# Inverting triangular blocks in 16x16 pieces, a PSUM bank of its own for preparation, and another order of two output parts in a hybrid decoder layer

## The chip, the cores and the metric

The kernel runs on one core of one Trainium2 chip. A core has a matrix engine (TensorE, "PE" in the profile), three engines for element-wise work (VectorE "DVE", ScalarE "ACT", GpSimd "POOL"), a sync engine that issues transfers (SyncE "SP"), and 16 DMA engines. Each engine works through its own queue in order and waits on semaphores for the others. The metric is the device time of one execution in microseconds; the median of several runs counts.

## The reference

The layer takes x of 256 tokens by 2048 channels, in fp32:

```python
x = LN1(alpha * x + 0.5 * SwiGLU_1(x))                  # 2048 -> 5632 -> 2048
x = LN2(alpha * x + W_out [DiffAttn(x) || RWKV7(x)])    # both from x @ W_in
x = LN3(alpha * x + 0.5 * SwiGLU_2(x))
```

DiffAttn has 8 heads with two score maps each. RWKV7 has 16 heads of size 64 with a state that is updated token by token:

```python
sa = einsum('bhvk,bhk->bhv', state, -kk_t)
state = state * w_t + sa * (kk_t * a_t) + v_t * k_t
y_t = einsum('bhvk,bhk->bhv', state, r_t)
```

After it come a group norm per head, a bonus term and a gate g = sigmoid(x W) g2.

## The kernel before, in words

**Weights.** Every weight matmul is computed in three parts at reduced precision: x and w are each split into a high part and a remainder. SP loads a raw piece of 256 rows by 512 columns (512 KB, L134, three buffers). ScalarE casts it to the high part `wh` (L137), VectorE subtracts to get `wl` (L138), and TensorE runs, for each 128x512 tile, high by high (L113), high by remainder (L114) and remainder by high (L115) into the PSUM tile `acc`. There are five to seven pairs `wh`/`wl` in rotation, and the second half of the tokens lags some pieces behind the first. In all there are 7968 such matmuls ("weight matmuls").

**Background.** The first feed-forward layer, the mixer and the second feed-forward layer follow each other. In the mixer the stream of weight pieces (first W_in, then W_out) carries the rest along: after each piece `run_bg` advances Python generators that emit the small work of RWKV (`rwkv_group`, `rwkv_values`) and attention (`attn_heads`), each with a credit per piece. When a part of W_out needs a result, `drain` runs generators until its own are done. A scheduler with a timeline model then settles the order on each engine; the queues are fixed in the built program.

**RWKV.** The 16 heads go in two groups of 8 (group 0, group 1). For each group: the low-rank decay and learning-rate matmuls with their sigmoids (L500, L501), cumulative sums, key norms with a logarithm and exponentials (L522, L523), the products of key and query sides `BK` and `AR` masked into `Q`; then the inversion. Each head has 4 chunks of 64 tokens, each chunk gives two triangular 32x32 blocks, so there are 64 blocks per group. ScalarE's queue sends them through memory (`dU`) so that one block lies on one partition, on 64 partitions. VectorE inverts them by a recurrence of 31 steps, a multiply (L583) and an add (L585) each. The inverses `Y` and the transposes go back through memory (`dY`, `dYT`) to the layout in which TensorE merges two 32x32 inverses into one of 64x64 (L608, L619; `TT`). L629 transposes `BK`. Then comes the chain of four chunks c = 0 to 3: L642 gives the right side `Rs`, L650 applies the inverse `TT`, L658 updates the state (not for the last chunk), L675 and L681 give the output, L682 copies it to `Yc`. Then the group norm (L696 sums, L700 square, L706 sums, L707 logarithm, L709 exponential, L711 to L716 on VectorE) and the gate (L727, L730, L731). The result is split in high part and remainder (L81, L82) and feeds W_out.

**Output.** `parts` lists the order in which W_out's input rows are taken: 0 and 1 are the halves of attention, 2 and 3 the groups of RWKV. Parts 0 and 2 go together (192 weight matmuls), then part 1 (96), then part 3 (96). After the last one, LN2 is finished; its constants are loaded by GpSimd (L209, L210) into buffers `J1` (that of `SV`, the values) and `Q`.

**PSUM.** Three tags serve the mixer beside `acc`: `at` with two banks (attention, transposes), `sm` with three (everything of RWKV).

Of the kernel before, what the change touches and what calls it, by code (L numbers as in the profile page):

```python
# [16 lines left out]
P = 128  # L17
# [16 lines left out]
BANKS = {"tr": ("at", 2), "sm": ("sm", 3), "at": ("at", 2)}  # L34
# [4 lines left out]
def build(tc, A, out):  # L39
# [49 lines left out]
    class Stream:  # L89
# [78 lines left out]
        def until(self, ready):  # L168
            idle = 0
            while not ready():  # L170
                assert idle < len(self.bg)
                g = self.bg.pop(0)
                try:
                    idle = idle + 1 if next(g) is None else 0
                    self.bg.append(g)
                except StopIteration:
                    pass

        def drain(self, gens):
            self.until(lambda: not any(g in self.bg for g in gens))  # L180
# [149 lines left out]
    def mix(mp, pq, C):  # L330
# [15 lines left out]


# [67 lines left out]
        def rwkv_cols(g, prev=None):  # L415
# [5 lines left out]
            stream.spawn(st["gen"], BG)  # L421

# [18 lines left out]
            return st  # L441
# [14 lines left out]
        def rwkv_values(g, st):  # L456
# [6 lines left out]
            for p in range(4):  # L463
                ps = bank("sm", (P, 4, P))
# [5 lines left out]
            ps = bank("sm", (P, 4, P))  # L470
# [4 lines left out]
            for hf in range(2):  # L475
                ps = bank("sm", (P, 2, S))
# [6 lines left out]
        def rwkv_group(g, st):  # L483
# [7 lines left out]
            for hf in range(2):  # L491
                pw = bank("sm", (P, 2, S))
                pl = bank("sm", (P, 2, S))
                for i in range(2):
                    c0 = (2 * hf + i) * P
                    T.matmul(pw[:, i, :], wa[0:64, c0:c0 + P], lora["tw"][0:64], start=True, stop=True)
                    T.matmul(pl[:, i, :], wa[64:128, c0:c0 + P], lora["tw"][64:128], start=True, stop=True)
                for i in range(2):
                    p = 2 * hf + i
                    SC.activation(out=tl[:, p, :], in_=pw[:, i, :], func=AF.Sigmoid, bias=col(0, g, p))  # L500
                    SC.activation(out=av[:, p], in_=pl[:, i, :].rearrange("p (c t) -> p c t", c=4), func=AF.Sigmoid, bias=col(1, g, p))  # L501
                yield 0.6
# [13 lines left out]
            for hf in range(2):  # L516
                ps = bank("sm", (P, 2, S))
# [32 lines left out]
            for p in range(4):  # L550
                pe = [bank("sm", (P, 4, P)) for e in range(2)]
# [8 lines left out]
            rk = t4("lw")  # L560
            for p in range(4):
# [5 lines left out]
            dY = dp.tile([64, 32, 32], F32, tag="dY", name=nm("dY"))  # L567
            dYT = dp.tile([32, 32, 32], F32, tag="dYT", name=nm("dYT"))
            quad = [(d, e, slice(64 * e + 32 * d, 64 * e + 32 * d + 32), slice(32 * d, 32 * d + 32),
                     slice(32 * d + 16 * e, 32 * d + 16 * e + 16)) for d in range(2) for e in range(2)]  # L570
            for d, e, rr, cc, uu in quad:
                nc.scalar.dma_start(out=dU[uu].rearrange("u s t -> s u t"),
                                    in_=Q[rr, :, :, e, cc].rearrange("p a c t -> p (a c) t"))
            U = hp.tile([64, 32, 32], F32, tag=HT["T1"], name=nm("U"))
            nc.scalar.dma_start(out=U, in_=dU)
            Y = hp.tile([64, 32, 32], F32, tag=HT["T2"], name=nm("Y"))
            V.memset(Y, 0.0)
            V.memset(Y.rearrange("p a b -> p (a b)")[:, ::33], 1.0)
            yield 0.6
            for j in range(31, 0, -1):  # L580
                tmp = mp.tile([64, 256], F32, tag="Rs", name=nm("itmp"))
                tv = tmp[:, 0:j * (32 - j)].rearrange("p (a b) -> p a b", a=j)
                V.tensor_tensor(out=tv, in0=U[:, 0:j, j:j + 1].to_broadcast([64, j, 32 - j]),  # L583
                                in1=Y[:, j:j + 1, j:32].to_broadcast([64, j, 32 - j]), op=ALU.mult)
                V.tensor_tensor(out=Y[:, 0:j, j:32], in0=Y[:, 0:j, j:32], in1=tv, op=ALU.add)  # L585
                if j % 2 == 0:
                    yield 1.0
            V.tensor_copy(out=U, in_=Y.rearrange("p a b -> p b a"))
            nc.scalar.dma_start(out=dY, in_=Y)
            nc.scalar.dma_start(out=dYT, in_=U[0:32])  # L590
            while "values" not in st:
                yield None
            SV = st["SV"]
            TT = hp.tile([P, 16, 64], F32, tag=HT["lw"], name=nm("TT"))
            G.memset(TT, 0.0)
            for d, e, rr, cc, uu in quad:
                nc.scalar.dma_start(out=TT[rr, :, cc], in_=dY[uu].rearrange("u s t -> s u t"))
            YT = hp.tile([P, 16, 32], F32, tag=HT["T1"], name=nm("YT"))
            PT = hp.tile([P, 16, 32], F32, tag=HT["T2"], name=nm("PT"))
            for e in range(2):  # L600
                nc.scalar.dma_start(out=YT[64 * e:64 * e + 32], in_=dYT[16 * e:16 * e + 16].rearrange("u s t -> s u t"))
            yield 0.6
            Qf = Q.rearrange("p a c e t -> p (a c) e t")
# [356 lines left out]
```

## Time and profile before

| | |
|---|---|
| runs | 2024.72, 2017.95, 2019.30 us |
| median | 2019.3 us |
| the profiled execution's own time | 2024.08 us |
| its span in the trace | 2022.2 us |
| TensorE busy | 1977.3 us, 98% |
| VectorE busy | 1147.5 us, 57% |
| ScalarE busy | 883.7 us, 44% |
| GpSimd busy | 35.7 us, 2% |
| mean granted clock of TensorE | 0.984 |

The span runs from the first to the last instruction in the trace; the execution's own time is about 2 us longer. Lines of the profile name the line of the kernel (L113), the engine, the operation, output and input by the program's names, and the shape. "PEld" is TensorE loading the stationary operand, "ACTq" a transfer that ScalarE's queue issued. The bracket at the end of a timeline row is the engine's idle time just before the instruction and what ended it. The granted clock is the share of full speed at which the throttle let TensorE run.

### The profile page before, as it was taken

How to read it: one execution, taken by the hardware profiler on the slowest of the kernel's cores; microseconds unless marked ns; L12 is line 12 of the kernel's file. 1: busy time of each engine (PE TensorE's matmuls, PEld its weight loads, DVE VectorE, ACT ScalarE, POOL GpSimd, SP SyncE). 2: the span in 40 equal slices, each digit the busy share in tenths (PEclk: the TensorE clock that was granted, in tenths of full speed). 3: DMA queues.
4: the chain of work that ended last, by engine and by line, in shares of the span. 5: the costliest groups of instructions: out<-in, count | busy, mean ns of one | idle time of the engine just before them, and what ended most of it. 6: DMA issues, size and time to landing. Idle time of an engine off the chain costs nothing. (4 is left out here: it accounts for less than half of the span.)

```text
span 2022.2 us, 24923 instructions
## 1 busy us (share of the span) xinstructions
PE 1977.3 (98%) x9671; PEld 1623.3 (80%) x9671; DVE 1147.5 (57%) x1419; ACT 883.7 (44%) x1095; POOL 35.7 (2%) x68
## 2 busy tenths in 40 slices
PE   9999999999999999999999988899999999999997
PEld 7888888888888878887777766788888888888886
DVE  5555554445545566775767865755555444555555
ACT  5444433344443335645574443444444334444432
POOL 0200000000000000000000000000000000000000
PEclk9999999999999999999999978999999999999999
DMA  7766666667666656565444624666665666766663
GB/s 243 218 188 195 185 191 209 207 193 229 192 188 188 196 163 196 160 176 163 136 121 141 207 63 154 194 203 187 189 195 185 206 208 198 230 188 189 187 194 129
DMA packets 202009, 373.35 MB, mean 185 GB/s; under 512 B 22827, under 2 KB 24945, under 8 KB 201121
## 3 DMA queue, kind: packets, MB, share of 16 engines
q1 hardware_dynamic: 182928, 350.53, 57.9%
q10 hardware_dynamic: 17440, 14.29, 2.5%
q0 software_dynamic: 1520, 6.93, 1.0%
q8 instruction: 76, 1.25, 0.3%
q14 instruction: 45, 0.36, 0.1%
HBM read 364.10 MB, written 7.60 MB: 184 GB/s over the span
## 5 line engine op out<-in xcount | busy, mean ns | idle before, releaser
L138 DVE TENSOR_TENSOR wl<-raw,wh 128x1024 fp32r<-128x1024 f32 (+1 forms) x665 | 808.0, 1216 | 670.3 <-ACT wh L137 669.3
L137 ACT CAST wh<-raw 128x1024 fp32r<-128x1024 f32 (+1 forms) x665 | 695.4, 1047 | 848.8 <-PE acc L115 733.6
L115 PE MATMUL acc<-wh,xl 128*128 128x512 f32 (+1 forms) x1952 | 741.8, 392 | 0.5 <-DVE xl L82 0.5
L114 PE MATMUL acc<-wl,xh 128*128 128x512 f32 (+1 forms) x1952 | 737.4, 393 | 0.7 <-DVE wl L138 0.7
L113 PE MATMUL acc<-wh,xh 128*128 128x512 f32 (+1 forms) x1952 | 725.5, 392 | 8.5 <-ACT xh L81 5.6
L113 PEld LDWEIGHTS acc<-wh,xh 128*128 128x128 f32 x1952 | 368.9, 189 | 87.5 <-ACT xh L81 7.1
L115 PEld LDWEIGHTS acc<-wh,xl 128*128 128x128 f32 x1952 | 368.9, 189 | 77.2 <-issue 2.0
L114 PEld LDWEIGHTS acc<-wl,xh 128*128 128x128 f32 x1952 | 369.0, 189 | 76.6 <-DVE wl L138 1.8
L115 PE MATMUL acc<-wh,hh 128*128 128x512 f32 x704 | 254.4, 390 | 0.0
L114 PE MATMUL acc<-wl,hh 128*128 128x512 f32 x704 | 253.5, 389 | 0.0
L113 PE MATMUL acc<-wh,hh 128*128 128x512 f32 x704 | 252.8, 389 | 0.0
L114 PEld LDWEIGHTS acc<-wl,hh 128*128 128x128 f32 x704 | 132.2, 188 | 27.6
L113 PEld LDWEIGHTS acc<-wh,hh 128*128 128x128 f32 x704 | 132.1, 188 | 27.4
L115 PEld LDWEIGHTS acc<-wh,hh 128*128 128x128 f32 x704 | 132.2, 188 | 27.3
L243 DVE TENSOR_TENSOR hh<-tr,hh 128x512 fp32r<-128x512 f32 x44 | 30.4, 691 | 64.1 <-ACT hh L242 64.1
L242 ACT CAST hh<-tr 128x512 fp32r<-128x512 f32 x44 | 25.8, 586 | 91.2 <-PE tr L232 91.2
L229 DVE SCALAR_TENSOR_TENSOR h<-sg,acc 128x512 f32<-128x512 f32 x44 | 30.2, 687 | 34.7 <-PE acc L115 34.7
L224 ACT ACTIVATE sg<-acc 128x512 f32<-128x512 f32 x44 | 26.3, 598 | 43.5 <-PE acc L115 43.5
L232 PEld LDWEIGHTS tr<-ident,h 128*128 128x128 f32 x176 | 21.9, 140 | 5.7
L232 PE MATMUL tr<-ident,h 128*128 128x128 f32 x176 | 26.3, 272 | 0.0
L583 DVE TENSOR_TENSOR itmp<-U,Y 64x31 f32<-64x31 f32 (+15 forms) x62 | 20.6, 333 | 4.1 <-DMA U<-dU 2.8
L585 DVE TENSOR_TENSOR Y<-Y,itmp 64x31 f32<-64x31 f32 (+15 forms) x62 | 20.6, 332 | 1.3
(239 smaller groups left out, 753.2 us busy)
## 6 DMA issues: line engine op xcount, KB each, us to landing
raw<-in_ffn_w_up_dram SPq DMA_DIRECT2D x176, 512.0 KB, 3.9
raw<-in_ffn_w_down_dram SPq DMA_DIRECT2D x176, 512.0 KB, 4.3
raw<-in_ffn_w_gate_dram SPq DMA_DIRECT2D x175, 512.0 KB, 3.9
raw<-in_w_in_dram SPq DMA_DIRECT2D x96, 512.0 KB, 3.7
raw<-in_w_out_dram SPq DMA_DIRECT2D x32, 512.0 KB, 4.1
xs<-y ACTq DMA_DIRECT2D x16, 256.0 KB, 3.3
rc<-xs ACTq DMA_DIRECT2D x16, 256.0 KB, 4.4
lng<-in_ln_g_dram POOLq DMA_DIRECT2D x3, 1024.0 KB, 7.8
```

Source lines behind the costliest of these rows:

```text
L113: T.matmul(a, hi, wh[:, j, :w], start=(ki + j == 0), stop=False)
L114: T.matmul(a, hi, wl[:, j, :w], start=False, stop=False)
L115: T.matmul(a, lo, wh[:, j, :w], start=False, stop=(ki + j == last))
L137: SC.copy(out=wh[:, c, :w], in_=raw[:, c, :w])
L138: V.tensor_tensor(out=wl[:, c, :w], in0=raw[:, c, :w], in1=wh[:, c, :w].bitcast(F32), op=ALU.subtract)
L224: SC.activation(out=s, in_=acc, func=AF.Silu)
L229: V.scalar_tensor_tensor(out=h, in0=sg[tt], scalar=0.5, in1=acc, op0=ALU.mult, op1=ALU.mult)
L232: T.transpose(tr[:, i, :], h[:, i * P:(i + 1) * P], ident)
L242: SC.copy(out=hi, in_=tr)
L243: V.tensor_tensor(out=lo, in0=tr, in1=hi.bitcast(F32), op=ALU.subtract)
L583: V.tensor_tensor(out=tv, in0=U[:, 0:j, j:j + 1].to_broadcast([64, j, 32 - j]), in1=Y[:, j:j + 1, j:32].to_broadcast([64, j, 32 - j]), op= ...
L585: V.tensor_tensor(out=Y[:, 0:j, j:32], in0=Y[:, 0:j, j:32], in1=tv, op=ALU.add)
```

## The change

Five things change together.

- Inversion (in `rwkv_group`): the blocks are cut to 16x16 on 128 partitions, so the recurrence has 15 steps (L599, L601 after). The two diagonal 16x16 blocks of each 32x32 block go through memory with runs of 16 numbers, in 2 DMAs for `U`, 4 for `dY` and `dYT` (L607) and 8 back (L613). `dY` and `dYT` are four tensors that GpSimd's queue fills with zeros once at the start of the mixer. TensorE then merges 16x16 to 32x32 by three sets of products (L618 64, L627 32, L633 64 matmuls per group), with copies and one addition around them. The old merges follow as before (L642 and L653 after, L608 and L619 before).
- Banks: `sm` has two banks, and a new tag `pr` one; the low-rank matmuls, the key norms, half of every second `Q` product and the transposes of the values use `pr`.
- Start: `rwkv_start` starts group 1's generator ahead of the attention columns, not with its own columns. The wait for the values stands behind the inversion.
- `drain` advances only the generators that it was asked for, and others only when these cannot go on.
- `parts` is (0, 2), (3,), (1,).

```diff
-BANKS = {"tr": ("at", 2), "sm": ("sm", 3), "at": ("at", 2)}
+BANKS = {"tr": ("at", 2), "sm": ("sm", 2), "pr": ("pr", 1), "at": ("at", 2)}
...
+        def advance(self, g):
+            try:
+                return next(g) is not None
+            except StopIteration:
+                self.bg.remove(g)
+                return True
 
         def drain(self, gens):
-            self.until(lambda: not any(g in self.bg for g in gens))
+            while any(g in self.bg for g in gens):
+                if not any([self.advance(g) for g in gens if g in self.bg]):
+                    assert any([self.advance(g) for g in self.bg if g not in gens])
...
+        zeroed = [[dp.tile([64, 32, 32], F32, tag=f"{n}{g}", name=f"{n}{g}") for n in ("dY", "dYT")] for g in range(2)]
+        zr = mp.tile([64, 256], F32, tag="Rs", name="zr")
+        G.memset(zr, 0.0)
+        for x in (t for z in zeroed for t in z):
+            nc.gpsimd.dma_start(out=x.rearrange("u (q s) t -> u q (s t)", q=4), in_=zr[:, None, :].to_broadcast([64, 4, 256]))
...
-                pw = bank("sm", (P, 2, S))
-                pl = bank("sm", (P, 2, S))
...
+                for k in range(2):
+                    ps = bank("pr", (P, 2, S))
...
-                pe = [bank("sm", (P, 4, P)) for e in range(2)]
+                pe = [bank("sm", (P, 4, P)), bank(("sm", "pr")[p % 2], (P, 4, P))]
...
-            for j in range(31, 0, -1):
...
+            for pp, ss in sub:
+                nc.scalar.dma_start(out=U[pp], in_=dU[:, ss, ss])
...
+            for j in range(15, 0, -1):
...
+            V.tensor_copy(out=YT, in_=Y.rearrange("p a b -> p b a"))
+            for dst, x in ((dY, Y), (dYT, YT)):
+                for pp, ss in sub:
+                    nc.scalar.dma_start(out=dst[:, ss, ss], in_=x[pp])
...
+            for dst, src in ((DT, dYT), (D, dY)):
+                for d, e, rr, cc, uu in quad:
+                    nc.scalar.dma_start(out=dst[rr], in_=src[uu].rearrange("u s t -> s u t"))
+            yield 0.6
+            ps = bank("sm", (P, 16, 32))
+            for u in range(16):
+                for d, e, rr, cc, uu in quad:
+                    T.matmul(ps[rr, u, :], UM[rr, u, :], DT[rr, u, :], start=True, stop=True)
+            V.tensor_tensor(out=PT, in0=ps, in1=C["id32"][:, None, :].to_broadcast([P, 16, 32]), op=ALU.add)
...
+                    T.matmul(ps[r, u, :], D[r, u, :], PT[r, u, :], start=True, stop=True)
+            V.tensor_copy(out=UM[0:32], in_=ps[0:32])
+            SC.copy(out=UM[64:96], in_=ps[64:96])
...
+                    T.matmul(ps[rr, u, :], PT[rr, u, :], D[rr, u, :], start=True, stop=True)
             for d, e, rr, cc, uu in quad:
+                (V.tensor_copy if e else SC.copy)(out=TT[rr, :, cc], in_=ps[rr])
...
-        r1 = rwkv_cols(0)
+        r1 = rwkv_start(0)
+        rwkv_cols(0, r1)
+        r2 = rwkv_start(1, r1)
         a1 = attn_cols(0)
-        r2 = rwkv_cols(1, r1)
+        rwkv_cols(1, r2)
...
-        parts = [(0, 2), (1,), (3,)]
+        parts = [(0, 2), (3,), (1,)]
```

The change moves instructions on every engine. Three places carry the prediction. The first is TensorE's queue at the last weight matmul of output part (0, 2). `sm` and `at` are small PSUM tiles, `k` and `qq` belong to the second attention half. Before, this follows it:

```order
L115 MATMUL acc_9640<-wh_9668,xl_9150 128x512
L619 MATMUL sm_8507<-TT_8441,PT_8448 32x32
L629 MATMUL sm_8544<-ident,BK_7242 128x64 x8
L829 MATMUL at_9414<-ident,ot_9319 128x128 x2
L774 MATMUL at_9441<-k_8144,qq 128x128
L774 MATMUL at_9441<-k_8144,qq 128x256
L619 MATMUL sm_8507<-TT_8441,PT_8448 32x32 x31
L629 MATMUL sm_8554<-ident,BK_7242 128x64 x8
```

After the change the same place reads as follows (L687 is the former L650, L695 the former L658, L712 and L718 the former L675 and L681, L679 the former L642, L832 and L838 attention):

```order
L115 MATMUL acc_9908<-wh_9936,xl_9418 128x512
L687 MATMUL sm_8924<-Rs_8904,TT_8409 64x64 x8
L695 MATMUL sm_8935<-SV_8638,BT_8696 64x64 x4
L695 MATMUL sm_8935<-SV_8638,BT_8697 64x64 x4
L712 MATMUL sm_8968<-Q,SV_8638 64x64 x8
L718 MATMUL sm_8968<-AR_6346,St_8872 64x64 x8
L832 MATMUL at_9822<-ident,s_9717 128x128
```

Before, group 1's merge and its whole chain stood behind the first output part; now the queue is in the third chunk (c = 2) of the chain there, and everything ahead of it stands among weight matmuls.

The second place is the group norm of group 1 and its gate, up to the next weight matmul, on TensorE. Before:

```order
L696 MATMUL sm_8890<-BK_7242,bones 128x256 x2
L696 MATMUL sm_8920<-BK_7242,bones 128x256 x2
L115 MATMUL acc_9831<-wh_9846,xl_9697 128x512
L114 MATMUL acc_9838<-wl_9807,xh_9700 128x512
L115 MATMUL acc_9838<-wh_9806,xl_9701 128x512
L706 MATMUL sm_8925<-BK_7242,bones 128x256 x2
L706 MATMUL sm_8929<-BK_7242,bones 128x256 x2
L727 MATMUL sm_8986<-gs_5667,g_1652_8887 128x256 x2
```

After (L733 is the former L696, L743 the former L706, L764 and L767 the former L727 and L730, L866 the last transpose of an attention head):

```order
L718 MATMUL sm_9027<-AR_6346,St_8944 64x64 x8
L866 MATMUL at_9956<-ident,ot_9872 128x128 x2
L733 MATMUL sm_9048<-BK_6347,bones 128x256 x2
L733 MATMUL sm_9052<-BK_6347,bones 128x256 x2
L866 MATMUL at_9960<-ident,ot_9886 128x128 x2
L743 MATMUL sm_9076<-BK_6347,bones 128x256 x2
L743 MATMUL sm_9080<-BK_6347,bones 128x256 x2
L764 MATMUL sm_9129<-gs_5679,g_1599_9045 128x256 x2
L767 MATMUL sm_9129<-gs_5680,g_1599_9045 128x256 x2
L764 MATMUL sm_9135<-gs_5679,g_1599_9045 128x256 x2
L767 MATMUL sm_9135<-gs_5680,g_1599_9045 128x256 x2
L113 MATMUL acc_9982<-wh_9977,xh_9964 128x512
```

Before, the norm came behind the matmuls of part (1,), with part (3,) waiting for it; now it follows the chain directly, still ahead of both remaining parts.

The third place is ScalarE's queue at the round trip of group 1's inverses through memory. Before:

```order
L589 DMA dY_8063<-Y_8071 64x1024
L137 CAST wh_9668<-raw_9667 128x1024
L590 DMA dYT_8064<-U_8069 32x1024
L597 DMA TT_8441<-dY_8063 32x16x32 x4
L601 DMA YT_8447<-dYT_8064 32x16x32 x2
L811 ACTIVATE ot_9319,ss_9320<-at_9315 128x128 x2
L137 CAST wh_9705<-raw_9704 128x1024
```

After:

```order
L607 DMA dY_5471<-W_8206 64x16x16 x2
L607 DMA dYT_5472<-W_8206 64x16x16 x2
L785 COPY k_8322<-tr_9260 128x4x128
L137 CAST wh_9340<-raw_9339 128x1024
L81 CAST xh_9409<-qq 128x512
L482 COPY SV_8638<-pr_8667 64x4x64
L613 DMA W_8313<-dYT_5472 32x16x32 x4
L613 DMA W_8313<-dY_5471 32x16x32 x4
L137 CAST wh_9358<-raw_9357 128x1024
```

Where one write stood before the loads there are now four writes, some casts and copies, and eight loads; the trip stands earlier in the stream, among the last pieces of W_in's and the first of W_out's columns. On TensorE, L618, the first product of the merge, stands among weight matmuls and waits for these loads; L627 and L633 follow 18 weight matmuls behind it. On GpSimd, the loads of LN2's constants (L207, L208 after) now stand ahead of the last power (L855) of the second attention half, behind all such powers before.

More of the change, by code (lines that the diff above doesn't have):

```diff
@@ L632, in rwkv_group @@
             st["cols"] = True
+            while "values" not in st:
+                yield None
+            SV = st["SV"]
             Yc = be
```

105 lines of the change are left out of this document (51 added, 54 removed).

## The prediction

> **What bounds the kernel now.** I read the spans and clocks first, then the page's busy times, then TensorE's timeline, then a table of busy times by stretch, and last the timeline inside the stretches that came out of line. The span is that of the profiled execution, whose own time is 2024.1 us; the median of the three runs is 2019.3, 0.24% less, so what I work out on the trace is scaled by 2019.3/2024.1 at the end.
>
> ```profile
> core 0: 2022.2 us, clock 0.984
> PE 1977.3 (98%) x9671; PEld 1623.3 (80%) x9671; DVE 1147.5 (57%) x1419; ACT 883.7 (44%) x1095; POOL 35.7 (2%) x68
> 1160.78 0.39 PE L115 MATMUL acc<-wh,xl 128*128 128x512 f32 x1
> 1162.60 0.39 PE L114 MATMUL acc<-wl,xh 128*128 128x512 f32 x1
> 735.00:1063.00 328.00, 321.89 (x1929) 261.42 (x1928) 231.75 (x404) 187.63 (x303) 7.04 (x7) 0.99 0.55 159
> 1063.00:1076.00 13.00, 11.24 (x50) 8.89 (x49) 12.97 (x17) 3.99 (x5) 0.00 (x0) 0.74 0.50 161
> 1164.00:1201.00 37.00, 29.10 (x370) 23.84 (x364) 25.92 (x77) 17.75 (x52) 4.03 (x3) 0.69 0.23 73
> 1201.00:1224.00 23.00, 23.00 (x147) 17.87 (x148) 10.61 (x14) 6.21 (x8) 1.14 (x2) 0.99 0.33 103
> 1224.00:1247.00 23.00, 15.84 (x51) 11.62 (x50) 11.25 (x17) 9.14 (x11) 0.00 (x0) 0.78 0.37 140
> ```
>
> TensorE is the bound: busy 98%, with VectorE at 57% and ScalarE at 44%. Its weight matmuls follow each other every 0.227 us: the two timeline rows are eight matmuls apart, (1162.60 − 1160.78)/8 (a record lasts 0.39, since they overlap). So the time changes in two ways only: TensorE gets more or less to do, or it gets other stretches in which no weight matmul is ready. The rows by stretch (start:end and length, then busy us and records of PE, its weight loads, VectorE, ScalarE, GpSimd, then granted clock, DMA share, GB/s) show three such stretches in the mixer: a short one at 1063, a long one from 1164 to 1201, and one after 1224. Each also has a low granted clock, 0.69 to 0.78 against 0.99.
>
> **The order of the output parts and what remains uncovered.** These rows give the weight matmuls' first stage (L113) alone, then the ends of both stretches.
>
> ```profile
> 1164.00:1201.00 37.00, 0.27 (x1) 0.27 (x1) 0.69 0.23 73
> 1201.00:1224.00 23.00, 11.14 (x28) 5.07 (x28) 0.99 0.33 103
> 1164.04 0.49 PE L115 MATMUL acc<-wh,xl 128*128 128x512 f32 x1
> 1189.14 1.12 PE L650 MATMUL sm<-Rs,TT 64*64 64x64 f32 x16
> 1195.82 0.68 PE L650 MATMUL sm<-Rs,TT 64*64 64x64 f32 x16 [0.44 <-DVE Rs L644]
> 1200.73 0.79 PE L113 MATMUL acc<-wh,xh 128*128 128x512 f32 x1
> 1200.85 0.37 ACT L682 COPY BK<-sm 128x256 f32<-128x256 f32 x1 [1.58 <-PE sm L681]
> 1223.73 1.89 PE L696 MATMUL sm<-BK,bones 128*128 128x256 f32 x8
> 1225.92 0.40 PE L115 MATMUL acc<-wh,xl 128*128 128x512 f32 x1
> 1226.40 1.04 ACT L137 CAST wh<-raw 128x1024 fp32r<-128x1024 f32 x1 [3.46 <-PE acc L115]
> 1227.35 1.05 ACT L700 ACTIVATE BK<-BK 128x1024 f32<-128x1024 f32 x1
> 1228.45 3.34 PE L706 MATMUL sm<-BK,bones 128*128 128x256 f32 x8 [2.14 <-ACT BK L700]
> 1241.19 0.79 PE L113 MATMUL acc<-wh,xh 128*128 128x512 f32 x1 [5.03 <-ACT xh L81]
> ```
>
> Before, weight matmuls are absent from 1164.0 to 1200.7, 36.7 us, while the group-1 merges, three chunks of the chain and half of an attention pair run one after the other, and from 1226.1 to 1241.2, 15.1 us, while the group norm and the gate of group 1 run. Together 51.8 us. In the changed order, between the end of the first output part and the next weight matmul there stand the end of chunk 2, chunk 3, the rest of the second attention pair, and the norm with its gate; parts 3 and 1 then follow without a break. I price that chain at the pace it has today, uncovered. From the inverse's product in one chunk to that in the next it is 1195.8 − 1189.1 = 6.7 us, and from the last of these to the copy L682 at 1201.2 it is 5.4, less some 0.8 for the state update, which the last chunk lacks, by the spacing of its matmuls in that stretch (an estimate): 4.6. So 11.3 us for the chunks. The tail is 1241.19 − 1223.73 = 17.5 us, less the weight cast of 1.04 that stands ahead of the square on ScalarE: 16.4. Sum 27.7. The attention half runs beside it.
>
> What goes under cover still costs TensorE its work. The stretch 1201:1224 shows the price of a covered chunk: 28 triples of weight matmuls at 0.227 us are 19.1 of 23.0 us, so chunk 3 costs 3.9. The stretch 1164:1201 holds 29.10 us of busy time at clock 0.69, 20.1 at full clock; three chunks are 11.7 of these, and 8.4 or less is merges, transposes and attention. Two chunks and most of that move under cover, 7.8 + 6 to 8 = 14 to 16, chunk 3 moves out, −3.9: 10 to 12, and I take 11. The gain is 51.8 − 27.7 − 11 = 13 us. What could be late in there is bounded on both sides: if everything runs covered at the busy time of its matmuls alone and the tail meets an idle ScalarE, −20; if the attention half, now beside the norm on the same engines, ends last, −4.
>
> **More matmuls.** The inversion of 16x16 blocks needs three more products per group (L618 64, L627 32, L633 64 matmuls of 32x32), 160 for each of two groups, 640 records since each matmul leaves two.
>
> ```profile
> 1162.91 1.20 PE L608 MATMUL sm<-YT,Q 32*32 32x32 f32 x64
> L583 DVE TENSOR_TENSOR itmp<-U,Y 64x31 f32<-64x31 f32 (+15 forms) x62 | 20.6, 333 | 4.1 <-DMA U<-dU 2.8
> L585 DVE TENSOR_TENSOR Y<-Y,itmp 64x31 f32<-64x31 f32 (+15 forms) x62 | 20.6, 332 | 1.3
> ```
>
> The same shape stands in L608: 64 records from 1162.91 to the next matmul at 1164.04, 1.13 us, 17.7 ns each. 640 such are 11.3 us, all of it on TensorE among weight matmuls: +11. Ends: +7.5 if the blocks of all four quarters of the array overlap better than L608's two, +16 if they stand as singles among weight matmuls (L618 is split 2 and 62 at the second group). The Trainium skill, "TensorE: Matmul & The Clock Gate", section "Wait — 56ns, not 53.3ns?", says that start to start never falls below about 25 ns however small the matmul; by that the term would be an estimated 16 us. The trace disagrees: L608 goes at 17.7 ns a record.
>
> VectorE's recurrences shrink from 62 + 62 instructions and 41.2 us to 30 + 30; at about 0.33 us each this takes some 20 us from an engine that is idle 43% of the time. No weight matmul waits for it, so I cost it at nothing; where casts and subtractions compete it may add a microsecond to the next term.
>
> **The preparation of group 1 moves ahead.** In the 1063 stretch TensorE waits for casts.
>
> ```profile
> 1057.35 0.50 PE L113 MATMUL acc<-wh,xh 128*128 128x512 f32 x1 [0.81 <-ACT wh L137]
> 1065.02 0.39 PE L113 MATMUL acc<-wh,xh 128*128 128x512 f32 x1
> 1067.17 0.50 PE L113 MATMUL acc<-wh,xh 128*128 128x512 f32 x1 [1.76 <-ACT wh L137]
> 1049.81 1.28 ACT L522 ACT_TABLE_LOAD   x1
> 1053.53 1.28 ACT L523 ACT_TABLE_LOAD   x1
> 1033.99 0.84 ACT L500 ACTIVATE tl<-sm,vB 128x256 f32<-128x256 f32 x2
> ```
>
> ScalarE holds sigmoids, a logarithm and exponentials with their table loads for group 1 in one cluster from 1034 to 1056, falls behind with the weight casts, and TensorE loses 0.8 us ahead of 1057.35 and 1067.17 − 1065.02 − 0.23 = 1.9 us at the second stop, after which it goes at half clock: in the row 1063:1076 a clock of 0.74 over 13 us is 3.4 us lost. Together 6.1. With group 1 started ahead of the attention columns and taking a bank of its own, the sigmoids are done earlier. The logarithm and exponentials stay near group 0's norm, so not all of it goes: −5, between −6 and +2 (the 2.6 us of the two table loads, if they fall among group 0's norm and are not covered).
>
> **New waits.** The round trip through memory had 13 DMAs per group on ScalarE's queue and has 18 now, and L618 waits in TensorE's own queue for the loads of the blocks.
>
> ```profile
> 919.17 4.11 ACTq L601 DMA_DIRECT2D YT<-dYT  x2
> 923.38 1.05 ACT L137 CAST wh<-raw 128x1024 fp32r<-128x1024 f32 x1 [7.32 <-DMA YT<-dYT]
> 1156.31 2.35 ACTq L597 DMA_DIRECT2D TT<-dY  x4
> 1159.87 0.28 ACT L811 ACTIVATE ot<-at 128x128 f32<-128x128 f32 x1 [6.29 <-DMA TT<-dY]
> U<-dU ACTq DMA_DIRECT2D x2, 256.0 KB, 3.7
> TT<-dY ACTq DMA_DIRECT2D x8, 64.0 KB, 4.4
> ```
>
> Today ScalarE stands still for 7.3 and 6.3 us in the two round trips, with weight casts queued behind, and TensorE does not stop in either (the row 735:1063 has it busy 98%, full clock). The new trip has 18/13 as many issues, so the stand on ScalarE may be 9 to 10 us (an estimate), and the weights cast ahead cover most of it: +1, the 0.8 us stop of 1057 being the nearest row for casts that come a little late; from 0 to +13 (a rival below). The chain has two banks instead of three, so a product waits for the copy two products back; it waits for the copy just before it anyway, with 0.44 us of idle time ahead of L650 at 1195.82, so 0, at most one such wait per chunk and product, 1 us in the exposed chunks. The 1 MB of zeros that GpSimd's queue writes at the start of the mixer moves beside weight loads that take a DMA share of 0.55 there (row 735:1063): 0, at most +2.
>
> **Sum.** −13 + 11 − 5 + 1 = −6 us: 2018.1 on the profiled execution, and times 2019.3/2024.1 that is 2013.
>
> **The rivals.**
> *More than that.* If the four blocks of each product overlap, +7.5 stands for +11, and if the tail meets an idle ScalarE, −17 for −13: with −5 and +1 some −14 us, 2005. For it speaks that the products are issued in quarters in turn; against it, L608 was issued in halves in turn and took 17.7 ns all the same.
>
> *The round trip stops TensorE (slower).* The blocks now leave and come back in runs of 64 bytes, 16 numbers, where before they were 128 bytes or more, and L618 stands in TensorE's queue among weight matmuls with 18 of them between its last instruction and the next product. The rows show 4.4 us to landing for 128-byte runs (TT) and 3.7 for whole rows (U), so the length of a run cost little; none shows 64-byte runs. If the loads land 3 us after TensorE reaches L618, TensorE loses 3 us and, as after the 1.9 us at 1065, 3.4 us of half clock, at each of two groups: +13 on the forecast, +7 in all, 2026. It decides against me when the two stops together exceed some 6 us with what follows. The Trainium skill, "DMA: Bandwidth & Descriptors", section "Specifications", says that transfers below 512 bytes are read, modified and written; it speaks against these runs, but this trace gives 128-byte runs no later landing than 4.4 us against 3.7.
>
> *The exposed stretch hardly shortens.* On GpSimd the two loads of LN2's constants, which must wait for the last readers of the chain's buffers, now stand ahead of the last power that the attention half needs, and on TensorE that half's last transpose (L866) stands ahead of the norm's second sum (L743). If that detour ends last, the gain of the first term is 4, not 13: +3, 2022. Against it: the norm's own way to L743, 1228.45 − 1223.73 = 4.7 us, runs at the same time.
>
> **How the numbers follow.** The forecast has 0.5, more than that 0.18, the round trip 0.2, the hardly shortened stretch 0.12. About 0.3% or 6 us is what a measurement of this kernel can tell from no change. The forecast lies at that bound, so half of its chance is faster and most of the rest same. Faster: 0.28 + 0.17 = 0.45. Slower: 0.17 of the round trip and 0.06 from the unfavourable ends of the other two: 0.23. Same: 0.32. The range goes from 2001, a little beyond the second case, to 2027, a little beyond the third.
>
> **What would show it.** Right, if the profile after has one stretch without weight matmuls of 25 to 30 us between the first output part and the end of the mixer's stream, no stop near 1065, L618 at some 18 ns a record, and no idle time of TensorE ahead of L618 above 1 us. Wrong, if idle time ahead of L618 or its cast shows DMA as releaser with a low clock behind it, if the stretch lasts 36 us or more, or if L618, L627 and L633 take over 16 us in all.

## The result and the profile after

The changed kernel takes 2039.5 us (median of four runs, 2037.6 to 2040.3) against 2020.4 before: 1.0093 times the time, 95% interval 1.0078 to 1.0108. The forecast was 2013, the range 2001 to 2027: wrong in sign and outside the range. The profiled span grew from 2022.2 to 2037.4 us. Of a later run (products left out, whole rows) one execution of 6999 us is not counted in its ratio.

The page of the changed kernel, first busy times, then (from its list of queues) what was moved to load instructions (packets, MB, share):

```profile
PE 1982.6 (97%) x10311; PEld 1623.3 (80%) x10311; DVE 1124.2 (55%) x1364; ACT 891.6 (44%) x1110; POOL 40.0 (2%) x75
q8 instruction: 81, 1.33, 0.3%
```

TensorE has 640 records more, as forecast, and is busy 5.3 us longer; the rest of the 15 us of span is idle time or time at another pace. The clock as a whole is not where the loss lies: its mean is 0.990, against 0.984 before. What TensorE waited for (in total, times, longest):

```profile
PE acc L114 <- DVE wl L138: 6.1, 6, 3.1
PE sm L618 <- DMA W<-dYT: 5.7, 4, 2.2
PE acc L113 <- ACT xh L81: 4.9, 2, 4.7
...
PE sm L642 <- issue: 1.4, 1, 1.4
```

The stretches by busy time, in the columns of the prediction:

```profile
890.00:931.00 41.00, 36.84 (x585) 28.80 (x584) 18.13 (x26) 19.47 (x31) 0.00 (x0) 0.96 0.57 137
1210.00:1238.00 28.00, 17.44 (x182) 12.63 (x180) 19.13 (x50) 13.57 (x33) 3.19 (x4) 0.98 0.43 144
1238.00:1284.00 46.00, 45.44 (x189) 37.38 (x190) 29.47 (x38) 14.74 (x15) 0.82 (x1) 0.94 0.44 134
```

The second row is the stretch without weight matmuls. It is one where there were two, and at 28.5 us (from the start of the last weight matmul at 1210.07 to that of the next at 1238.56) close to the 27.7 that I had worked out; behind it parts 3 and 1 run without a break (third row). This part went as forecast. The first row is new: it holds the weight matmuls number 3700 to 3800, counted from the start, and group 0's merge. They took 41 us; before, the same hundred took 23.6 (885.3 to 908.9). TensorE's timeline there:

```profile
902.21 0.22 PE L618 MATMUL sm<-W,X 32*32 32x32 f32 x2 [0.43 <-DMA W<-dYT]
904.80 0.24 PE L618 MATMUL sm<-W,X 32*32 32x32 f32 x2 [1.94 <-DMA W<-dYT]
909.21 1.32 PE L618 MATMUL sm<-W,X 32*32 32x32 f32 x122
915.83 1.17 PE L627 MATMUL sm<-X,W 32*32 32x32 f32 x62
916.86 1.26 PE L633 MATMUL sm<-W,X 32*32 32x32 f32 x126
920.69 0.63 PE L642 MATMUL sm<-X,Q 32*32 32x32 f32 x27 [1.43 <-issue]
```

The products themselves are quick: 126 records of L633 in 1.26 us. But single L618s stand among weight matmuls and wait for the loads, and behind the long row of small products TensorE stops within L642 with no releaser ("issue"). The queue of transfers on ScalarE at the same time, and its transfers to landing (count, KB, us):

```profile
892.06 1.33 ACTq L607 DMA_DIRECT2D dY<-W  x2
893.52 3.91 ACTq L607 DMA_DIRECT2D dYT<-W  x2
899.96 1.94 ACTq L613 DMA_DIRECT2D W<-dYT  x4
901.93 4.54 ACTq L613 DMA_DIRECT2D W<-dY  x4
dY<-W ACTq DMA_DIRECT2D x4, 64.0 KB, 6.4
dYT<-W ACTq DMA_DIRECT2D x4, 64.0 KB, 6.0
```

The writes in runs of 64 bytes land after 6.0 to 6.4 us; before, 3.6 and 4.4 for two and four times the bytes. The Trainium skill, "DMA: Bandwidth & Descriptors", section "Specifications", says that a transfer below 512 bytes is read, modified and written. The later landing of these writes would fit that, but no row shows what the DMA does, and the writes in 128-byte runs before (`dU`, 64 KB) landed after 3.2 us.

The stop near 1065 moved and did not go. ScalarE, VectorE, then TensorE, in the changed kernel:

```profile
1040.70 1.04 ACT L137 CAST wh<-raw 128x1024 fp32r<-128x1024 f32 x1
1043.16 1.21 DVE L544 TENSOR_TENSOR BK<-BK,tl 64x1024 f32<-64x1024 f32 x1
1044.38 1.22 DVE L545 TENSOR_TENSOR BK<-BK,tl 64x1024 f32<-64x1024 f32 x1
1045.71 1.22 DVE L138 TENSOR_TENSOR wl<-raw,wh 128x1024 fp32r<-128x1024 f32 x1
1046.99 0.80 PE L114 MATMUL acc<-wl,xh 128*128 128x512 f32 x1 [3.15 <-DVE wl L138]
```

The cast for this piece was done at 1041.7, but group 1's preparation, now earlier, stood ahead of the subtraction. Half clock followed from 1046.0 to 1052.8, 3.4 us lost: some 6 us in all, as at the stop before (6.1).

### The profile page after: what moved, and what is told of

It is laid out like the page before. It is cut to its first block, busy times and chain, and to the rows that moved or that the text cites. A ratio compares the mean times of both kernels' runs of the same rounds, so it can differ in the third digit from the quotient of the medians.

```text
span 2037.4 us, 26209 instructions
## 1 busy us (share of the span) xinstructions
PE 1982.6 (97%) x10311; PEld 1623.3 (80%) x10311; DVE 1124.2 (55%) x1364; ACT 891.6 (44%) x1110; POOL 40.0 (2%) x75
## 4 chain that ended last, share of the span: by engine, by line
PE 88%; DVE 5%; DMA 3%; ACT 2%; issue 1%; ACTq 1%; POOL 0%; DVEq 0%
PE acc L113 27%; PE acc L114 27%; PE acc L115 27%; DVE wl L138 2%; PE tr L230 1%; DMA raw<-in_w_in_dram 1%; DVE y L193 1%; ACT wh L137 1%; DMA dYT<-W 1%; DMA raw<-in_ffn_w_up_dram 1%; PE at L811 1%; DVE y L194 0%; PE tr L361 0%; PE sm L564 0%; DMA raw<-in_w_out_dram 0%
## 5 line engine op out<-in xcount | busy, mean ns | idle before, releaser
L266 DVE TENSOR_TENSOR y<-y,acc 128x512 f32<-128x512 f32 x16 | 11.0, 685 | 16.9 <-PE acc L115 16.9
L367 ACT ACTIVATE df<-praw,vB 128x256 f32<-128x256 f32 (+1 forms) x27 | 13.7, 507 | 8.5 <-DVE vv L373 5.9
```

## The experiments

Each is told against the kernel before, timed beside it on the same chip (2018.9 to 2021.0), as a ratio with its interval. Between runs on different chips the medians can mislead by a few us; where it matters, the ratios are given too. My first theory after the result: the new inversion costs about 20 us (products 9, round trip 10), the moved preparation 6, the shorter stretch gives 15 back. The rivals: the part order, the early start.

**Old inversion, all else changed.**

```diff
-            for j in range(15, 0, -1):
...
+            for j in range(31, 0, -1):
...
```

The whole section of `rwkv_group` from `dU` to the old merge is that of before, with its trip through memory and without zero fill and products.

> The changed kernel with the old inversion (32x32 blocks on 64 partitions, 31 steps, no zero fill) and everything else as changed. Theory: of the 19 us by which the changed kernel is slower, 9.6 are the added products (their records in its trace take 4.4 + 2.0 + 3.2 us) and some 10 are stops of TensorE around L618 and behind it (6.1 us idle, 1.2 ahead of the old merge, 3.4 lost at half clock). Both go; the longer recurrence brings the chain later and leaves one more chunk uncovered, some +6. So -14 us against the changed kernel: 2025 us, no idle time at the merges above 1 us. Rival (the other output order or the early start of group 1 carries the loss): the inversion is a gain as meant, so without it 0 to +6 against the changed kernel: 2039 to 2046.

Measured: 2010.5 us, 0.9955 (0.9944 to 0.9967). The new inversion costs not 14 but 29 us here; without it the change is a gain. Its stretches:

```profile
889.00:915.00 26.00, 26.00 (x128) 21.58 (x128) 25.07 (x50) 13.73 (x22) 0.00 (x0) 1.00 0.61 172
1173.00:1210.00 37.00, 23.43 (x267) 17.39 (x266) 24.39 (x70) 17.86 (x50) 3.26 (x4) 0.92 0.30 104
```

The hundred weight matmuls of 41 us take 26 (the merge comes later, and TensorE's longest wait for its loads is 0.7 us), although the stretch behind the first part is 9 us longer than in the changed kernel (37.6).

**Old part order, all else changed.**

```diff
-        parts = [(0, 2), (3,), (1,)]
+        parts = [(0, 2), (1,), (3,)]
```

> The changed kernel with the output parts in the old order (0,2), (1,), (3,). Theory: the shorter exposed stretch comes from the chain starting earlier, not from the new order; with part 1 next, its weight matmuls can start when the attention half is split, ahead of the second half of the norm and of the gate, which then lie under them. The exposed stretch falls from 28.7 to some 18 us: -10 us against the changed kernel, 2029. Rival (the new order is what shortened it): a second exposed stretch of 10 to 15 us comes back ahead of part 3: 0 to +5 against the changed kernel, 2039 to 2044.

Measured: 2029.6 us, 1.0053 (1.0040 to 1.0066), as the theory said. Weight matmuls start right behind the norm's second sum, and the gate lies among them:

```profile
1222.32 1.99 PE L743 MATMUL sm<-BK,bones 128*128 128x256 f32 x8
1223.96 0.58 PE L113 MATMUL acc<-wh,xh 128*128 128x512 f32 x1
...
1229.19 1.03 PE L764 MATMUL sm<-gs,g 128*128 128x256 f32 x4
```

**Writes in whole rows.**

```diff
-            for dst, x in ((dY, Y), (dYT, YT)):
-                for pp, ss in sub:
-                    nc.scalar.dma_start(out=dst[:, ss, ss], in_=x[pp])
+            for pp, ss in sub:
+                V.tensor_copy(out=Z[pp, 1, :, ss], in_=Y[pp].rearrange("p a b -> p b a"))
+                V.tensor_copy(out=Z[pp, 0, :, ss], in_=Y[pp])
+            for dst, n in ((dYT, 1), (dY, 0)):
+                for pp, ss in sub:
+                    nc.scalar.dma_start(out=dst[:, ss, :], in_=Z[pp, n])
```

> The changed kernel, but each 16x16 inverse is copied on VectorE into a zero-padded tile (four small copies per group in place of one), and the four writes per group go out in whole rows of 32 numbers, 2 KB in one run, in place of runs of 64 bytes; the zero fill through memory is gone. Theory: the writes in 64-byte runs, 6.0 to 6.4 us to landing in the changed kernel against 4.4 and 3.6 for the writes before, make the loads late and so stop TensorE at L618. The landing falls to some 4 us, the idle time ahead of L618 from 6.1 to under 2 us and its half clock goes: -7 us against the changed kernel, 2032. Rival (the time goes into issuing so many DMAs from ScalarE's queue, and in the order of the instructions, whatever the runs): idle time ahead of L618 above 4 us, 2037 to 2042.

Measured: 2034.6 us, 1.0074 (1.0061 to 1.0087), 5 us less. The landing fell as forecast:

```profile
dYT<-Z ACTq DMA_DIRECT2D x4, 128.0 KB, 3.7
dY<-Z ACTq DMA_DIRECT2D x4, 128.0 KB, 3.6
```

Twice the bytes land in 60% of the time. The waits for the loads at L618 fell from 5.7 to 1.7 us, and 1.5 us came up there with no releaser. The edit also puts the writes of `dYT`, whose loads the first product needs, ahead of those of `dY`; how much of the shorter wait comes from that was not run apart.

**Late start of group 1, all else changed.**

```diff
-        r2 = rwkv_start(1, r1)
         a1 = attn_cols(0)
+        r2 = rwkv_start(1, r1)
         rwkv_cols(1, r2)
```

> The changed kernel with group 1's generator started with its own columns, behind the attention columns, as before the change. Theory: the preparation of group 1 no longer stands ahead of the casts and subtractions at the place where TensorE stopped for 3.1 us in the changed kernel (a subtraction behind three 1.2 us operations of the preparation), but makes the stops of before at its old place: -3 us against the changed kernel, between -7 and +2; 2036. Rival (the early start carries the loss): -15 us or more, 2024.

Measured: 2040.9 us, 1.0109 (1.0094 to 1.0125). The 3.1 us stop went (the longest wait for a subtraction is 1.2), but the waits ahead of L618 grew from 5.7 to 9.4. That is 5 us from the theory's 2036, though inside its bounds, and against the rival. In the changed kernel the early start is thus worth 1.4 us.

**Old inversion and old part order.** Both diffs above together.

> The changed kernel with the old inversion and with the output parts in the old order too; of the change there stay the early start of group 1, the bank for preparation, the new drain. Theory: the two effects add, since they lie at different places (the inversion's trip, the stretch behind the first output part): the old order lets part 1 cover the norm's second half and the gate, -9 to -12 us as in the run with the old order alone: 1999 us against 2010.5 with the old inversion alone. Rival (with the longer inversion the chain ends later and the attention half is not ready, so part 1 covers nothing): 2007 to 2011.

Measured: 2004.2 us, 0.9906 (0.9890 to 0.9923): faster than both kernels, and between theory and rival. The gain of the order is 6 us by the medians and 10 by the ratios.

**The kernel before with the new inversion alone.** The inversion of the change, its zero fill, the later wait for the values and the other buffer for one product (`rk`) put into the kernel before.

> The kernel before with nothing changed but the inversion (16x16 blocks, zero fill, products, the wait for the values behind it, the buffer that this needs). Theory: TensorE gets 9 us of products and 8 to 10 us of stops and half clock at the round trip; the chain starts earlier, so that the 36.7 us without weight matmuls shrink by 20 or so, of which some 14 come back as work under cover: +10 us against the kernel before, 2029. Rival (the loss came from how the inversion meets the other edits, the early start above all): 2013 or less, the shorter stretch being a gain.

Measured: 2032.0 us, 1.0048 (1.0033 to 1.0063): +11, as the theory said. The new inversion loses without the other edits too, but 11 us, not 29. The trace shows why: the new inversion alone brings the chain forward, and the first stretch without weight matmuls falls from 36.7 to 10.1 us:

```profile
1201.17 0.39 PE L115 MATMUL acc<-wh,xl 128*128 128x512 f32 x1
1211.27 0.50 PE L113 MATMUL acc<-wh,xh 128*128 128x512 f32 x1
```

So the new inversion and the early start shorten the same stretch, and what each gains alone doesn't add up.

**Old inversion, late start, new part order.**

> The changed kernel with the old inversion and with group 1 started with its own columns, as before. Theory (the early start is worth little by itself, as the run with the late start alone showed, +1.5 us): 2011 to 2016, the stops for casts near 1060 being back at 2 to 6 us. Rival (the early start is what made the run with the old inversion 9 us faster than the kernel before): 2017 to 2021.

Measured: 2016.3 us, 0.9977 (0.9967 to 0.9986), 6 us behind the same with the early start (4 by the ratios): at the upper edge of the theory's 2011 to 2016, and short of the rival.

**Products doubled**, in each of the three sets (the first is shown).

```diff
+                    for _ in range(2):
                         T.matmul(ps[rr, u, :], UM[rr, u, :], DT[rr, u, :], start=True, stop=True)
```

> The changed kernel with each of the three new sets of products issued twice into the same place, 320 instructions and 640 records more. Theory: the records cost what their start to start says, 4.4 us for 320: +9 us against the changed kernel, 2048, with the stops ahead of L618 as they were. Rival A (the array works on four blocks at a time and the cost lies in switching between shapes, once per set): +2 us or less, 2041. Rival B (25 ns a record): +16 us, 2055.

Measured: 2055.8 us, 1.0169 (1.0154 to 1.0185): +16, rival B's figure, but by luck and not by its mechanism. The records of the three sets took 19.3 us against 8.6 (start to start, without pauses over 0.6 us; 13.6 against 7.5 when time at half clock counts half), so +6 to +11 where the theory had +9, and 11 to 15 ns a record, not 25. On top come stops in the midst of a set, and half clock behind them; other waits became shorter:

```profile
917.64 1.24 PE L636 MATMUL sm<-W,X 32*32 32x32 f32 x109
921.65 1.97 PE L636 MATMUL sm<-W,X 32*32 32x32 f32 x128 [2.78 <-issue]
925.11 0.37 PE L636 MATMUL sm<-W,X 32*32 32x32 f32 x11 [1.48 <-issue]
```

TensorE stops every 128 records, with no semaphore that it waits for. The stretch of weight matmuls 3700 to 3800 now reads 54 us at clock 0.84:

```profile
886.00:940.00 54.00, 44.83 (x905) 36.67 (x905) 17.21 (x25) 20.08 (x31) 0.00 (x0) 0.84 0.43 104
```

**Three shared banks**, on the old inversion and the old order.

```diff
-BANKS = {"tr": ("at", 2), "sm": ("sm", 2), "pr": ("pr", 1), "at": ("at", 2)}
+BANKS = {"tr": ("at", 2), "sm": ("sm", 3), "pr": ("sm", 3), "at": ("at", 2)}
```

> The fastest version so far (old inversion, old part order, 2004 us) with three banks that preparation and chain share, as before, in place of two and one of its own. Theory: the bank of its own lets group 1's preparation run beside group 0's chain; without it the chain of group 1 starts later (its first product with the inverse now stands behind the first output part, where it stood ahead of it), one more chunk is uncovered: +6 us, 2010. Rival (the bank is worth nothing, two banks for the chain cost what the third gives): 2002 to 2006.

Measured: 2003.0 us, 0.9907 (0.9895 to 0.9920). The rival holds: the bank is worth nothing.

**The new inversion mended.** Whole rows, old order, and pauses between loads and products (`for _ in range(6): yield 1.6`).

> The changed kernel with the new inversion kept and what the runs so far found mended: writes in whole rows from a padded tile, the old part order; the generator also pauses for six pieces between the loads and the products. Theory: 2034.6 with the long runs, less the 10 us of the part order, less one chunk that now lies under weight matmuls (the queue is in the fourth chunk at the end of the first output part): 2019 to 2024. It stays 15 us or more behind the same kernel with the old inversion (2004), since 9 us of products, their waits and the stops remain. Rival (the products are cheap and the new inversion only suffered from its writes): 2000 to 2008.

Measured: 2024.0 us, 1.0018 (1.0009 to 1.0027): 20 us behind the old inversion, at the upper end of the theory's range.

**The kernel before with the new part order alone.**

> The kernel before with nothing changed but the order of the output parts. Theory: the order by itself is a loss: chunk 3 and the tail of group 1 lose part 1 as their cover; the 36.7 and 15.1 us without weight matmuls and chunk 3's 3.9 under cover become 36.7 + 6 + 16.4 in one stretch: +4 us, 2023 to 2025. Rival (one stretch is better than two, since each stop brings half clock): 2012 to 2016.

Measured: 2020.6 us, 1.0001 (0.9991 to 1.0010). Neither: the order alone is worth nothing. The trace has the one stretch of the theory, 60 us for two of together 51.8, but it cost no time.

**No early start**, on the three shared banks.

> The version with the old inversion, the old part order and three shared banks (2003 us), but with group 1 started with its own columns, as before the change. Of the change there is left only the wait for the values behind the inversion, the buffer of one product and the new drain. Theory: the early start of group 1 is the one gain of the change, 17 us by itself: 2019 to 2022, as the kernel before, with the two stretches without weight matmuls back at 37 and 15 us. Rival (the wait moved behind the inversion carries it, the early start only the 6 us that it made between the two runs with the new part order): 2007 to 2010.

Measured: 2020.5 us, 1.0000 (0.9991 to 1.0010), against 2003.0 with the early start. With the old inversion and the old order, the early start alone is a gain of 17.5 us. The wait for the values behind the inversion, the other buffer and the new `drain` are no part of it: this run has all three and takes the time of the kernel before. The gain hangs on the company: 4 to 6 us with the old inversion and the new order, 1.4 with the new inversion and the new order.

**Few wide products, without and with whole rows.** Each set as 4, 2 and 4 products of 32x512.

```diff
-                    T.matmul(ps[rr, u, :], UM[rr, u, :], DT[rr, u, :], start=True, stop=True)
+                T.matmul(ps[rr], UM[rr, 0, :], DT[rr], start=True, stop=True)
```

> The changed kernel with each set of 64 or 32 small products replaced by one product of 32x32 by 32x512 per block row (4, 2 and 4 instructions), which leaves out the use of each block's own factor: every block is multiplied with the first block's. Round trip, copies and waits stay. Theory: the 640 records cost 8.7 us and the 1.4 us of refetching ahead of the old merge; the stops ahead of the first product stay at 4 us or more with their half clock: -10 us against the changed kernel, 2029 to 2031. Rival (so many small instructions also hold up what stands around them, by fetching): -18 us or more, 2021.

> The same with the writes in whole rows from the padded tile. Theory: the two effects add, 2034.6 for the long runs less 10: 2024 to 2026, and 14 us remain to the version with the old inversion and the new part order (2010.5), for the longer round trip and what it delays. Rival (products with their fetching, and short writes, are all that the new inversion costs): 2008 to 2014.

Measured: 2031.2 us, 1.0072 (1.0056 to 1.0089), and 2035.0 us, 1.0083 (1.0069 to 1.0097). The first comes out at the upper end of the theory's range, for a wrong reason: a wide product took 0.94 us among weight matmuls, so TensorE was as busy as before (1984.7 us). The second misses both theory and rival: the waits ahead of the products are gone, and the stop behind group 1's preparation came back larger:

```profile
1043.75 0.80 PE L114 MATMUL acc<-wl,xh 128*128 128x512 f32 x1 [4.46 <-DVE wl L138]
```

**Products left out, without and with whole rows.** One 32x32 product per block row, into a cleared bank, in each of the three sets (the first is shown).

```diff
+            V.memset(ps, 0.0)
             for d, e, rr, cc, uu in quad:
-                    T.matmul(ps[rr, u, :], UM[rr, u, :], DT[rr, u, :], start=True, stop=True)
+                T.matmul(ps[rr, 0, :], UM[rr, 0, :], DT[rr, 0, :], start=True, stop=True)
```

> The changed kernel with one 32x32 product per block row in each set (4, 2 and 4 instructions in place of 64, 32 and 64) into a bank that VectorE clears: 300 of the 320 products are left out. Trip, copies and waits stay. It corrects the run with few wide products, which kept TensorE as busy (0.94 us for one wide product). Theory: -8.7 us of records, and the stop ahead of the old merge: -10 against the changed kernel, 2029; what is left over the version with the old inversion (2010.5) is the trip and what it delays, 19 us. Rival (the many small instructions cost more than their records): 2020 or less.

> The same with the writes in whole rows from the padded tile. Theory: no idle time ahead of the first product; a part of the remaining cost lies in stops at other places that depend on the order (the subtraction behind group 1's preparation near 1040 us): 2020 to 2028. Rival (products and short writes are all that the new inversion costs): 2008 to 2014.

Measured: 2018.8 us, 0.9999 (0.9988 to 1.0009), and 2020.4 us, 0.9997 (0.9987 to 1.0007). The rival holds in the first: leaving out 300 products gains 20.7 us, while their records are 6 to 7 us (the 7.5 to 8.6 above, less 1.7 of those that stay). The waits for the loads are still 4.7 us; the same hundred weight matmuls take 31 us, at full clock:

```profile
PE sm L618 <- DMA W<-dYT: 4.7, 2, 2.5
PE acc L114 <- DVE wl L138: 3.8, 5, 1.2
889.00:920.00 31.00, 28.81 (x212) 22.86 (x211) 14.48 (x17) 15.36 (x25) 0.00 (x0) 1.00 0.68 165
```

Not all of the gain belongs to the products: the stop for subtractions near 1040 us, some 6 us with its half clock in the changed kernel, is 1.0 and 0.8 us here, at full clock, so some 4 us of the 20.7 arose there. Whole rows bring no gain on top, as the second theory's lower end had it.

**The ladder.** One edit at a time, from the kernel before (the wait for the values, the buffer and the drain, which come with the first step, made no difference alone). By the ratios, on 2020 us, the steps are −19, 0, +10 and +28:

| version | us | step |
|---|---|---|
| before | 2020 | |
| + early start of group 1 | 2003.0 | −17 |
| + bank for preparation | 2004.2 | +1, no difference |
| + new part order | 2010.5 | +6 |
| + new inversion | 2039.5 | +29 |

Each step is worth this in this place only: on the kernel before, the new inversion cost 11 us, and in the changed kernel the early start gained 1.4.

## Why the prediction was wrong

The forecast was −6 and the change +19, 25 us apart. Three of the four terms failed: the products (priced by their records alone), the preparation (its stop moved and stayed as long) and the waits at the round trip (put at +1, 9 us in the trace). The length of the exposed stretch was right.

**The exposed stretch** (term −13): its length was right, 28.5 for 27.7 us. What brings the gain was not seen. I put it on the package and its part order. The early start of the chain brings it, which the early start of group 1 and the new inversion each give; only the first gives it without a price on TensorE. With the old inversion and the old order, the first stretch is 23.2 us and the second is gone:

```profile
1169.36 0.40 PE L115 MATMUL acc<-wh,xl 128*128 128x512 f32 x1
...
1192.53 0.50 PE L113 MATMUL acc<-wh,xh 128*128 128x512 f32 x1
```

That row pair is of the version with three shared banks. The new order takes part 1 away as cover for the norm and gate, 6 to 10 us once the chain starts early.

**More matmuls** (term +11): a failed step, mis-sized. The records are 7.5 to 8.6 us, less than I had. But doubling them costs 16 us and leaving them out gains 21, or 16.5 without the 4 near 1040: a small product costs some 50 to 55 ns, all told (16.4/320 and 16.5/300, an estimate, since other waits change with the order too), where the row gave 2 x 17.7. Only 1.4 us of the difference is a stop behind the sets in the changed kernel (L642); how the rest divides stays open. I priced the set by the records of L608 and stopped reading at the weight matmul behind it. The next small product behind that one, L619, stood with 3.2 us of idle time and "issue" as its releaser, and I took that for a part of the exposed stretch:

```profile
1167.70 0.28 PE L619 MATMUL sm<-TT,PT 32*32 32x32 f32 x2 [3.17 <-issue]
```

The rule of the Trainium skill that I set aside ("TensorE: Matmul & The Clock Gate", section "Wait — 56ns, not 53.3ns?": no start to start below some 25 ns) gave an estimated 16 us. The sum agrees with the doubled run, the mechanism doesn't, since the 1280 records there came at 11 to 15 ns each.

**The preparation moves ahead** (term −5): failed in the changed kernel, where the stop moved from 1065 to 1043 with 3.15 us of waiting, some 6 us with its half clock as before, so nothing was gained. With the old inversion it does go: the fastest version waits 1.0 us in all for subtractions. How long it is depends on where the scheduler puts the preparation: 1.0 us there, 7.7 in the run with wide products and whole rows.

**New waits** (term +1): 5.7 us ahead of L618, and half clock at 906 to 909.5 and 1127.9 to 1131.3, 3.4 us lost. The slower rival named the place and the waiting (3 us at each group) well; the half clock was 1.7 at each for its 3.4, and the measured loss is 9 us instead of 13. That writes in short runs land later is shown (6.0 to 6.4 us against 3.6). What it costs in the end is not: whole rows gained 5 us in one variant and nothing in two others, because other stops took the place.

Put together by the ladder, the early start gives −17, the bank +1, the order +6 and the new inversion +29: the 19 us. Of the 29 the products are 16 to 21; the 8 to 13 that remain, for the round trip and what it displaces, are the difference and were not measured apart. How they divide stays open: the scheduler lays every variant out anew, and a stop taken away at one place came back at another.

## What to carry to other kernels

Price a set of very small instructions by doubling it or leaving it out, not by its records alone, see in both traces which other stops moved with it, and in the profile read on to the next instructions of the same engine: a stop with no releaser behind such a set belongs to its price. When a change bundles edits, ask of each what it does alone and what it does beside the others: here one edit of five could make the whole gain, but hardly any of it beside the new inversion, and work taken off an idle engine (VectorE's recurrence, 20 us) and put on the bound one cost more than all the others gave. A block of output that is ready early can cover what is late, so it goes ahead of the late one; here that was worth 6 to 10 us with the early start and nothing in the kernel before.

## What the runs showed of the hardware that I had not expected

TensorE, given a row of small instructions without a break, stops for 1 to 3 us about every 128 records, with no semaphore as releaser. The instruction loads fit that: 76 packets before, 81 in the changed kernel, 86 with the products doubled and 76 with them left out, which is TensorE's records (9671, 10311, 10951, 9711) divided by 128 and rounded up, at 16.4 KB a packet. The page of the run with products doubled:

```profile
q8 instruction: 86, 1.41, 0.3%
```

The packets' own times in the trace fit too. In that run they lie at 919.50 to 920.46 and 922.79 to 923.91 us, and the stops within L636 end at 921.65 and 925.11. All seven such stops at its merges (six of them within the sets), and the one at L642 in the changed kernel, end 1.1 to 1.5 us after a packet has ended (at L619 in the kernel before it is 0.1 us). So the stops are very likely waits for instructions; no row names the releaser.

A short stop can cost more than its length, but need not. In the kernel before, 1.76 us of waiting at 1067 was followed by 6.8 us at half clock, and in the changed one 1.94 us at 905 by 3.4; with the products left out, two waits of 2.2 and 2.5 us ahead of L618 were followed by none. In the doubled run TensorE ran at half clock for 68.8 us in all against 41.4 in the changed kernel, which is 13.7 us more lost.
